# Sums of weight quarters made by accumulating transfers on POOL's queue instead of by VectorE

## The chip, the cores and the metric

The kernel runs on one core of one Trainium2 chip. The metric is the device time of one execution in microseconds; the number that counts is the median of several runs.

## The reference, cut to what matters

A block of a streaming encoder: 16 learned tokens are put ahead of 1024 frames of width 1024. A mixer (four mLSTM heads and four retention heads) is projected back by `w_out`; a gated MLP with a causal convolution over three tokens follows, whose last product is with `w_down`.

```python
mixed = jnp.concatenate([h_ml, h_rt], axis=-1)          # (L, 2048)
h = h + mixed @ w_out                                   # w_out (2048, 1024)
...
a = causal_dwconv(u @ w_up, ffn_conv_w)
h = h + (silu(a) * (u @ w_gate)) @ w_down               # w_down (2816, 1024)
```

All is float32. The change touches only how the two products with `w_out` and `w_down` get their weights.

## The kernel before, in words

**Stages.** The input is loaded and normed in four pieces of tokens (144, 256, 384, 256). Then the heads run one after the other in the order 4, 0, 1, 2, 3, 5, 6, 7: projections of values (`v_group`, L411), of queries and keys (`qk_group`, L447) and of the output gate (`o_group`), with the chunked scan of the head (`scan_a`, `scan_b`) merged in between. Up to about 700 us the trace shows this part, then the product with `w_out`, then the MLP from 840 us or so, and from about 1300 us the product with `w_down`. Each float32 operand is split into a high and a low half that TensorE takes as fp32r, so a product is three matmuls: high by high, high by low, low by high.

**Seven products for eight.** The products with `w_out` and `w_down` (class `Seven`, L630) are done by a Strassen scheme in Winograd's form: left and right factor are cut into quarters, and seven products of quarters, or of sums of quarters, take the place of eight. With w11, w21, w12, w22 the quarters of the weights, the scheme needs four sums of them: w21 + w22, w21 - w11, w21 + w22 - w11 and w12 - (w21 + w22 - w11). The activations need sums of their own (`tsum`, L681, and the step "65" in `prep`, L708 to L715). `give` (L746) and `last_quarter` (L752) add the products into the residual `resid`.

**Weight sums before.** They are made per row block of 128 (8 blocks for `w_out`, KD = 11 for `w_down`) and put into tensors in HBM, `sums[g, st, k]` (L183), two of them (`65` and `73`) of 128 x 1024 floats for each block. SP's queue brings the quarters into SBUF, VectorE makes the four sums, and SP's queue writes them to HBM. For `w_out` that is `wsum` (L185): two loads, four instructions on 128 x 512, four stores, tied by `after` behind the last instruction of a query or key group. For `w_down` it is done in halves, 22 units of two loads, four instructions on 128 x 256 and two stores (`dload`, `dsum`, `dnext`, `dstep`, L198 to L234), called from `seven` (L1335) in the MLP; their buffers are `Rb` and one tile `dsum`. `Seven.load` (L657) later reads the sums back as any weight, on SP's queue.

**Order of the work.** The program is recorded in the order of the Python code; a scheduling layer then orders each engine's instructions by the data they depend on and by its own estimate of the time, and sets the semaphores. `after` gives it an order that it must keep. `ahead` (L251 to L255) says behind which query or key group of which head a `wsum` or a `first_right` is called. POOL does almost nothing: memsets at the start (L383 to L401) and two multiplications at the end (L1576). SP issues nearly all transfers, in order; a load that waits holds up those behind it. At the start SP's queue holds, in this order: the first piece of the input (L106), the first head's value weights (L142), the second piece (L1004), constants, the third piece, the two rotary tables (L576, L577), the fourth piece, a mask, and the first query and key weights.

Of the kernel before, what the change touches and what calls it, by code (L numbers as in the profile page):

```python
# [10 lines left out]
F32 = mybir.dt.float32  # L11
F32R = mybir.dt.float32r
AF = mybir.ActivationFunctionType
ALU = mybir.AluOpType
# [3 lines left out]
P = 128  # L18
# [10 lines left out]
NPAIR = NFB // 2  # L29
# [35 lines left out]
def body(ctx, tc, h_in, vecs, cst, mask_in, rot, w_v0, w_v, w_fm, w_out, w_up, w_gate, w_down, out):  # L65
# [117 lines left out]
    sums = {(g, st, k): dram.tile([P, 2 * HB], F32, name=f"ws{g}{st}_{k}") for g, n in (("w", 8), ("d", KD)) for st in ("65", "73") for k in range(n)}  # L183

    def wsum(g, k):  # L185
        src, n = (w_out, 8) if g == "w" else (w_down, KD)
        a, b = (accp.tile([P, 2 * HB], F32, tag=f"rr{i}", name=f"ws{g}{k}_{i}") for i in range(2))
        nc.sync.dma_start(a, src[k])
        nc.sync.dma_start(b, src[k + n])
        w11, w21, w12, w22 = a[:, :HB], a[:, HB:], b[:, :HB], b[:, HB:]  # L190
        after(nc.vector.tensor_tensor(w22, w21, w22, ALU.add), last["qk"])
        nc.vector.tensor_tensor(w21, w21, w11, ALU.subtract)
        nc.vector.tensor_tensor(w11, w22, w11, ALU.subtract)
        nc.vector.tensor_tensor(w12, w12, w11, ALU.subtract)
        for st, i, x in (("65", 0, w11), ("65", 1, w22), ("73", 0, w12), ("73", 1, w21)):
            nc.sync.dma_start(sums[g, st, k][:, i * HB:(i + 1) * HB], x)

    def dload(k, q, x):  # L198

        n = HB // 2  # L200
        b = x.rearrange("p (a b j) -> p a b j", a=2, b=2)
        for i in range(2):
            nc.sync.dma_start(b[:, :, i], w_down[k + i * KD].rearrange("p (a j) -> p a j", a=2)[:, :, q * n:(q + 1) * n])

    def dsum(k, q, x, prev):

        n = HB // 2
        w11, w12, w21, w22 = (x[:, i * n:(i + 1) * n] for i in range(4))
        after(V.tensor_tensor(w22, w21, w22, ALU.add), prev)
        V.tensor_tensor(w21, w21, w11, ALU.subtract)  # L210
        V.tensor_tensor(w11, w22, w11, ALU.subtract)
        V.tensor_tensor(w12, w12, w11, ALU.subtract)
        for st, i, j in (("65", 0, 4), ("73", 1, 3)):
            nc.sync.dma_start(sums["d", st, k].rearrange("p (a j) -> p a j", a=2)[:, :, q * n:(q + 1) * n],
                              x.rearrange("p (i j) -> p i j", i=4)[:, i:j:3 if st == "65" else 1])

    dcount = [0, 0]
    dunits = [(k, q) for k in range(KD) for q in range(2)]
    dbufs = []

    def dnext():

        if len(dunits) > dcount[1]:
            x = dbufs[dcount[1] % 2] or fp4.tile([P, 2 * HB], F32, tag="dsum", name=f"dsum{dcount[1]}", bufs=1)
            dopen.append((*dunits[dcount[1]], x))
            dload(*dopen[-1])
            dcount[1] += 1

    dopen = []

    def dstep(x):
        if dopen:
            dsum(*dopen.pop(0), x)
            dnext()  # L234
# [6 lines left out]
    def first_right(k):  # L241
        a = accp.tile([P, 2 * HB], F32, tag="rr0", name=f"fr{k}")
        r = accp.tile([P, 2 * HB], F32R, tag="rr1", name=f"frs{k}")
        nc.sync.dma_start(a, mxd[k])
        nc.scalar.copy(r[:, :HB], a[:, :HB])
        after(nc.vector.tensor_tensor(r[:, HB:], a[:, :HB], r[:, :HB].bitcast(F32), ALU.subtract), last["qk"])
        nc.vector.tensor_tensor(a[:, HB:], a[:, HB:], a[:, :HB], ALU.subtract)
        nc.sync.dma_start(rone[k], r.bitcast(F32))
        nc.sync.dma_start(diff[k], a[:, HB:])

    ahead = {(g, "q", 0): [lambda k=k: wsum("w", k)] for k, g in enumerate((1, 2, 3, 5, 6, 7))}  # L251
    for k, g in ((6, 6), (7, 7)):
        ahead[g, "k", 1] = [lambda k=k: wsum("w", k)]
    for k in range(8):
        ahead[5 + k // 3, *(("q", 1), ("q", 2), ("k", 0))[k % 3]] = [lambda k=k: first_right(k)]  # L255

# [373 lines left out]
    class Seven:  # L630
# [48 lines left out]
                self.nload += 1  # L679

        def tsum(self, i, k):  # L681
            a, b, c = {1: ("A1", "B1", "A1"), 3: ("B1", "B1", "B2")}[i]
            return V.tensor_tensor(self.act[a, k], self.act[b, k], self.act[c, k], ALU.subtract)

        def prep(self, t):

            if t >= len(self.steps) or t in self.ops:
                return
            st, k = self.steps[t]
            nm = f"{self.nm}{st}_{k}"  # L690
            d = self.draws.get(t, {})
            act = self.act
            if st == "4" and self.order[-1] != "4":
                if t not in self.four:
                    self.pre4(t)
                r = rsplit(act["A1", k], self.rt(st, k, 0))
                self.ops[t] = [(self.four[t], r, "x")]
            elif st == self.order[-1]:
                if k % 2 == 0:
                    self.w = d.get("w")  # L700
                w = self.four.get(t) or wsplit(*self.wlast(k), [self.w[:, k % 2 * HB:(k % 2 + 1) * HB]])
                self.ops[t] = [(w, self.rhalf(k, 0), "xy"[st == "2"])]
            elif st in self.QUARTER:
                if k % 2 == 0:
                    self.w = fsplit(nm, [d["w"]])
                r = self.right.get((st, k)) or rsplit(act[{"1": "A1", "2": "A2", "4": "A1"}[st], k], self.rt(st, k, 0))
                self.ops[t] = [(half_of(self.w, k % 2), r, "xy"[st == "2"])]
            elif st == "65":  # L708
                a1, a2, b2 = (act[q, k] for q in ("A1", "A2", "B2"))
                r5 = rsplit(a1, self.rt(st, k, 1))  # L710
                V.tensor_tensor(a1, b2, a1, ALU.subtract)
                w = fsplit(nm, [d["l"]])
                r6 = rsplit(a1, self.rt(st, k, 0))
                V.tensor_tensor(a1, a2, a1, ALU.subtract)
                self.ops[t] = [(half_of(w, 0), r6, "x"), (half_of(w, 1), r5, "y")]  # L715
            else:
                w = fsplit(nm, [d["l"]])
                r7 = rsplit(act["B1", k], self.rt(st, k, 0))
                r3 = rsplit(act["B2", k], self.rt(st, k, 1))
                self.ops[t] = [(half_of(w, 1), r7, "x"), (half_of(w, 0), r3, "y")]  # L720
            self.read(t)
# [339 lines left out]
    for i, h in enumerate(HEADS):  # L1061
# [240 lines left out]
    def seven(kind, i, chunks, done):  # L1302
# [6 lines left out]
        for n, (bank, s, o, x) in enumerate(PROD):  # L1309
            hi, lo = need((kind, i, s), 2)  # L1310
            xs = xb(x)
            for ci, (j0, j1) in enumerate(chunks):
# [13 lines left out]
                if n in (0, 2, 3):  # L1326
                    if ci == 0:
                        S[n] = ftile(f"s{n}{kind}{i}")
                    nc.scalar.copy(S[n][:, w], pt)
                else:  # L1330
                    t = {1: 0, 4: 3, 5: 2}.get(n)
                    if t is not None:
                        x = nc.vector.tensor_tensor(S[t][:, w], pt, S[t][:, w], ALU.add)
                        if n != 4 and ci == len(chunks) - 1:
                            dstep(x)  # L1335
            if n == 1:
                done(0, 0, S[0])
            elif n == 4:
# [142 lines left out]
    for i in range(1, NPAIR):  # L1481
        u, g = up_part(i), gate_part(i)
        next(u)
        if i == 1:
            next(g)
        run(u)
        if i == NPAIR - 1:
            for t in range(4):
                down.load(t)
        run(g)  # L1490
        if 2 < i:
            kb = i - 3
            nc.sync.dma_start(resid[:, kb, META:], stream[:, kb])
        if i < 5:
            first_out((i - 1) % 2, (i - 1) // 2)
        if i == 4:
            fseg4.close()
            fp4 = fseg4.enter_context(tc.tile_pool(name="fp5", bufs=1, side="right"))
            dbufs += [Rb[:, :2 * HB], None]
            dnext()  # L1500
            dnext()

    for k in range(KD):
        aload("A1", k)
    down.prep(0)
    for k in range(KD - 1):
        aload("A2", k)
    assert not dopen
    fseg4.close()
    fseg2.close()  # L1510
    fseg.close()
# [172 lines left out]
```

## Time and profile before

| | |
|---|---|
| Median of 3 runs | 1537.58 us (1537.52 to 1537.78) |
| Span of the profiled execution | 1536.0 us |
| TensorE matmuls busy | 98% of the span |
| VectorE busy | 74% |
| ScalarE busy | 48% |
| POOL busy | 0%, 13 instructions |
| HBM read, written | 155.89 MB, 55.62 MB |
| Granted TensorE clock | 0.99 to 1.00 up to the last 16 us |

The span reaches from the first to the last instruction of the program in the profiled execution; what the runs have beyond it, 1.6 us, lies around it. A row of a group gives line, engine, operation, the tile written and the tiles read, the count, then busy time in us, the mean of one in ns, and the idle time of the engine ahead of it. A row of waits reads: who waited, for whom, us in total, times, the longest. In the rows of transfers stand the size of one in KB and the us from issue to landing.

### The profile page before, as it was taken

What the parts mean: (1) busy time and instruction counts of PE and PEld (TensorE: products, weight loads), DVE (VectorE), ACT (ScalarE), POOL (GpSimd) and SP (SyncE); (2) the same over time, 40 slices, a digit from 0 to 9 for tenths busy, and PEclk for the clock granted to TensorE, in tenths of its full rate; (3) what the DMA queues carried; (4) which work ended last, traced back from release to release, by engine and by line L of the source; (5) the groups of instructions that cost most, each with busy time, mean ns of one, the idle gap of its engine ahead of it and who ended that gap; (6) DMA issues with size and microseconds to landing.
All of it is one profiled execution on the core that took longest, in us unless ns stands there. A gap on an engine that the chain in (4) does not pass through costs nothing.

```text
span 1536.0 us, 25538 instructions
## 1 busy us (share of the span) xinstructions
PE 1512.7 (98%) x9753; PEld 1392.8 (91%) x9753; DVE 1131.5 (74%) x2443; ACT 743.2 (48%) x1491; POOL 2.5 (0%) x13
## 2 busy tenths in 40 slices
PE   7999999999999999999999999999999999999997
PEld 7989999999999999998788998999999999888887
DVE  8757767686867677687966788677777777778657
ACT  7374555555542534434454465444444444344443
POOL 0000000000000000000000000000000000000000
PEclk9999999999999999999999999999999999999999
DMA  6131231332425346278542245323465656933313
GB/s 216 42 98 63 70 122 65 109 112 80 141 67 184 126 131 209 91 249 305 184 146 97 83 129 181 102 93 101 155 193 167 198 186 230 366 109 104 96 42 111
DMA packets 111771, 213.18 MB, mean 139 GB/s; under 512 B 9944, under 2 KB 54688, under 8 KB 111648
## 3 DMA queue, kind: packets, MB, share of 16 engines
q1 hardware_dynamic: 111504, 211.48, 41.8%
q8 instruction: 76, 1.25, 0.3%
q14 instruction: 47, 0.39, 0.1%
q10 hardware_dynamic: 144, 0.07, 0.0%
HBM read 155.89 MB, written 55.62 MB: 138 GB/s over the span
## 4 chain that ended last, share of the span: by engine, by line
PE 95%; DMA 2%; DVE 2%; ACT 1%; issue 0%; DVEq 0%; ACTq 0%
PE pv L431 4%; PE pv L432 4%; PE pv L433 4%; PE po L442 4%; PE po L441 4%; PE po L443 4%; PE pdx L608 3%; PE pdx L610 3%; PE pdx L609 3%; PE pup_x L609 2%; PE pup_x L610 2%; PE pga_x L608 2%; PE pga_x L610 2%; PE pga_x L609 2%; PE pup_x L608 2%; PE pdy L608 2%
## 5 line engine op out<-in xcount | busy, mean ns | idle before, releaser
L431 PE MATMUL pv<-hi_v,uh 128*128 128x256 f32 (+1 forms) x512 | 147.2, 288 | 7.7 <-ACT hi_v L145 7.7
L432 PE MATMUL pv<-lo_v,uh 128*128 128x256 f32 (+1 forms) x512 | 145.9, 286 | 0.0
L433 PE MATMUL pv<-hi_v,ul 128*128 128x256 f32 (+1 forms) x512 | 145.6, 285 | 0.0
L441 PE MATMUL po<-uh,hi_o 128*128 128x386 f32 (+2 forms) x384 | 125.1, 326 | 0.0
L442 PE MATMUL po<-ul,hi_o 128*128 128x386 f32 (+2 forms) x384 | 122.8, 320 | 0.0
L443 PE MATMUL po<-uh,lo_o 128*128 128x386 f32 (+2 forms) x384 | 122.6, 319 | 0.0
L431 PEld LDWEIGHTS pv<-hi_v,uh 128*128 128x128 f32 x512 | 97.2, 190 | 10.5 <-ACT hi_v L145 7.7
L432 PEld LDWEIGHTS pv<-lo_v,uh 128*128 128x128 f32 x512 | 96.9, 190 | 0.9 <-DVE lo_v L146 0.8
L433 PEld LDWEIGHTS pv<-hi_v,ul 128*128 128x128 f32 x512 | 96.9, 190 | 0.1
L299 ACT CAST hi_up<-raw_up 128x512 fp32r<-128x512 f32 (+1 forms) x52 | 36.5, 719 | 105.7 <-PE pga_z L609 60.7
L441 PEld LDWEIGHTS po<-uh,hi_o 128*128 128x128 f32 x384 | 72.5, 189 | 0.1
L442 PEld LDWEIGHTS po<-ul,hi_o 128*128 128x128 f32 x384 | 72.4, 189 | 0.1
L443 PEld LDWEIGHTS po<-uh,lo_o 128*128 128x128 f32 x384 | 72.2, 188 | 0.1
L608 PE MATMUL pup_x<-uh_g,hi_up 128*128 128x256 f32 (+1 forms) x240 | 67.2, 282 | 0.4 <-ACT uh_g L1096 0.4
L609 PE MATMUL pup_x<-ul_g,hi_up 128*128 128x256 f32 (+1 forms) x240 | 67.4, 283 | 0.1
L610 PE MATMUL pup_x<-uh_g,lo_up 128*128 128x256 f32 (+1 forms) x240 | 66.3, 282 | 0.0
L300 DVE TENSOR_TENSOR lo_ga<-fraw_ga,hi_ga 128x512 fp32r<-128x512 f32 (+1 forms) x52 | 41.9, 808 | 32.2 <-ACT hi_ga L299 32.1
L300 DVE TENSOR_TENSOR lo_d<-rd,hi_d 128x1024 fp32r<-128x1024 f32 (+1 forms) x34 | 37.7, 1112 | 34.8 <-ACT hi_d L299 34.8
L441 PE MATMUL pq<-uh,hi_q 128*128 128x400 f32 (+2 forms) x192 | 62.1, 323 | 1.0 <-DVE qT L472 0.9
L442 PE MATMUL pk<-ul,hi_k 128*128 128x400 f32 (+2 forms) x192 | 62.1, 324 | 0.0
L441 PE MATMUL pk<-uh,hi_k 128*128 128x400 f32 (+2 forms) x192 | 62.0, 323 | 0.0
L443 PE MATMUL pq<-uh,lo_q 128*128 128x400 f32 (+2 forms) x192 | 62.0, 323 | 0.0
(757 smaller groups left out, 4978.7 us busy)
## 6 DMA issues: line engine op xcount, KB each, us to landing
raw_up<-w_up_d SPq DMA_DIRECT2D x22, 512.0 KB, 3.6
fraw_ga<-w_gate_d SPq DMA_DIRECT2D x22, 512.0 KB, 4.5
acts<-cv SPq DMA_DIRECT2D x44, 256.0 KB, 3.5
rd<-wsd SPq DMA_DIRECT2D x22, 512.0 KB, 3.5
raw_o<-w_fm_d SPq DMA_DIRECT2D x16, 512.0 KB, 3.5
wsw<-w_out_d SPq DMA_DIRECT2D x16, 512.0 KB, 3.8
wsw<-wsw SPq DMA_DIRECT2D x32, 256.0 KB, 2.1
raw_v<-w_v_d SPq DMA_DIRECT2D x14, 512.0 KB, 3.7
```

The lines of the kernel that those rows point to most:

```text
L299: nc.scalar.copy(hi[:, o:o + n], x)
L300: nc.vector.tensor_tensor(lo[:, o:o + n], x, hi[:, o:o + n].bitcast(F32), ALU.subtract)
L431: nc.tensor.matmul(pv[:L, :nv], a, hi[:, o:o + nv], start=kb == 0, stop=False)
L432: nc.tensor.matmul(pv[:L, :nv], a, lo[:, o:o + nv], start=False, stop=False)
L433: nc.tensor.matmul(pv[:L, :nv], b, hi[:, o:o + nv], start=False, stop=kb == KB - 1)
L441: nc.tensor.matmul(pt[:, :n], a, uh[kb][:, t0:t1], start=kb == 0, stop=False)
L442: nc.tensor.matmul(pt[:, :n], a, ul[kb][:, t0:t1], start=False, stop=False)
L443: nc.tensor.matmul(pt[:, :n], b, uh[kb][:, t0:t1], start=False, stop=kb == KB - 1)
L608: m.append(nc.tensor.matmul(pt, ah, xh_, start=first and k == 0, stop=False, skip_group_check=True))
L609: nc.tensor.matmul(pt, ah, xl_, start=False, stop=False, skip_group_check=True)
L610: m.append(nc.tensor.matmul(pt, al, xh_, start=False, stop=last and k == n - 1, skip_group_check=True))
```

## The change

One function `wsum(g, k)` makes the sums for both weights. It uses no SBUF and no VectorE: seven transfers on POOL's queue go from HBM to HBM, four of them accumulating (the target is read, the source added, the result written). Accumulation can only add here, so the sums are kept with plus signs only: the second half of `d65` becomes v21 + v22, where v are the quarters of the weights in the order of the listing, its first half v11 + v21 + v22, the second half of `d73` becomes v21 + v11, its first half v12 + v11 + v21 + v22. Where a sign has changed, the other factor is negated instead (`first_right`, `tsum`, step "65"), or the product is subtracted from the residual instead of added (`give`, `last_quarter`). What the mathematics needs of the original weights' signs comes out the same.

The first of the seven transfers waits for `last["pace"]`, an instruction of VectorE. `wsum("w", k)` is called at the same places as before; `wsum("d", k)` is called twice for each pair of the MLP, from pair 1, until the 11 blocks are used up. The transfers that follow the first are tied only by the data they read and write.

```diff
     def wsum(g, k):
+
         src, n = (w_out, 8) if g == "w" else (w_down, KD)
-        a, b = (accp.tile([P, 2 * HB], F32, tag=f"rr{i}", name=f"ws{g}{k}_{i}") for i in range(2))
-        nc.sync.dma_start(a, src[k])
-        nc.sync.dma_start(b, src[k + n])
-        w11, w21, w12, w22 = a[:, :HB], a[:, HB:], b[:, :HB], b[:, HB:]
-        after(nc.vector.tensor_tensor(w22, w21, w22, ALU.add), last["qk"])
-        nc.vector.tensor_tensor(w21, w21, w11, ALU.subtract)
-        nc.vector.tensor_tensor(w11, w22, w11, ALU.subtract)
-        nc.vector.tensor_tensor(w12, w12, w11, ALU.subtract)
-        for st, i, x in (("65", 0, w11), ("65", 1, w22), ("73", 0, w12), ("73", 1, w21)):
-            nc.sync.dma_start(sums[g, st, k][:, i * HB:(i + 1) * HB], x)
-
-    def dload(k, q, x):
...
+        d65, d73 = sums[g, "65", k], sums[g, "73", k]
+        v11, v21, v12, v22 = (src[k + i * n][:, o:o + HB] for i in range(2) for o in (0, HB))
+        dma = nc.gpsimd.dma_start
+        add = lambda x, y: dma(x, y, accum_op=ALU.add)
+        first = dma(d65, src[k])
+        tc.add_manual_dep(first.ins, last["pace"].ins.name, mybir.DependencyInfo(mybir.DependencyClass.Sync, mybir.DependencyReason.DATA), reason="pace")
+        dma(d73[:, HB:], v21)
+        dma(d73[:, :HB], v12)
+        add(d65[:, HB:], v22)
+        add(d73[:, HB:], v11)
+        add(d65[:, :HB], d65[:, HB:])
+        add(d73[:, :HB], d65[:, :HB])
...
-        nc.vector.tensor_tensor(a[:, HB:], a[:, HB:], a[:, :HB], ALU.subtract)
+        nc.vector.tensor_tensor(a[:, HB:], a[:, :HB], a[:, HB:], ALU.subtract)
...
-            a, b, c = {1: ("A1", "B1", "A1"), 3: ("B1", "B1", "B2")}[i]
+            a, b, c = {1: ("A1", "A1", "B1"), 3: ("B1", "B2", "B1")}[i]
...
-                V.tensor_tensor(a1, b2, a1, ALU.subtract)
+                V.scalar_tensor_tensor(a1, a1, -1.0, b2, ALU.mult, ALU.subtract)
...
-                V.tensor_tensor(a1, a2, a1, ALU.subtract)
+                V.scalar_tensor_tensor(a1, a1, -1.0, a2, ALU.mult, ALU.subtract)
...
-                    V.tensor_tensor(self.rs(j + j0, half), self.banks[b, j], self.rs(j + j0, half), ALU.add)
+                    x = self.rs(j + j0, half)
+                    V.tensor_tensor(x, x, self.banks[b, j], ALU.subtract if j0 else ALU.add)
...
-            V.tensor_tensor(x, pt, x, ALU.add)
+            V.tensor_tensor(x, x, pt, ALU.subtract if st == "4" else ALU.add)
...
                 qk_group(g, kind, p)
+                last["pace"] = last["qk"]
...
-                        x = nc.vector.tensor_tensor(S[t][:, w], pt, S[t][:, w], ALU.add)
-                        if n != 4 and ci == len(chunks) - 1:
-                            dstep(x)
+                        last["pace"] = nc.vector.tensor_tensor(S[t][:, w], pt, S[t][:, w], ALU.add)
...
         run(u)
+        if dsums and i < NPAIR - 1:
+            wsum("d", dsums.pop(0))
...
         run(g)
+        if dsums and i < NPAIR - 1:
+            wsum("d", dsums.pop(0))
```

The functions `dload`, `dsum`, `dnext` and `dstep` are gone, and with them the buffer `dsum` and the use of `Rb` for it.

More of the change, by code (lines that the diff above doesn't have):

```diff
@@ L194, in wsum @@
-        nc.vector.tensor_tensor(w12, w12, w11, ALU.subtract)
-        for st, i, x in (("65", 0, w11), ("65", 1, w22), ("73", 0, w12), ("73", 1, w21)):
-            nc.sync.dma_start(sums[g, st, k][:, i * HB:(i + 1) * HB], x)
-    def dload(k, q, x):
[L200 to L234, printed above, removed]
+        d65, d73 = sums[g, "65", k], sums[g, "73", k]
@@ L238, in body @@
+        add(d73[:, :HB], d65[:, :HB])
+    dcount = [0]
     rone = [dram.tile([P, 2 * HB], F32, name=f"rone{k}") for k in range(8)]
@@ L253, in body @@
         ahead[g, "k", 1] = [lambda k=k: wsum("w", k)]
+    dsums = list(range(KD))
     for k in range(8):
@@ L1498, in body @@
             fp4 = fseg4.enter_context(tc.tile_pool(name="fp5", bufs=1, side="right"))
-            dbufs += [Rb[:, :2 * HB], None]
-            dnext()
-            dnext()
     for k in range(KD):
@@ L1507, in body @@
         aload("A2", k)
-    assert not dopen
     fseg4.close()
```

## The prediction

> **What bounds the kernel now.** I read the page's first part, then TensorE's own waits, then busy time by stretches, and last the transfers of the start.
>
> ```profile
> span 1536.0 us, 25538 instructions
> PE 1512.7 (98%) x9753; PEld 1392.8 (91%) x9753; DVE 1131.5 (74%) x2443; ACT 743.2 (48%) x1491; POOL 2.5 (0%) x13
> ```
>
> ```profile
> PE pv L431 <- ACT hi_v L145: 7.7, 1, 7.7
> PE u L878 <- DVE C L916: 1.0, 1, 1.0
> PE pq L441 <- DVE qT L472: 0.9, 1, 0.9
> ```
>
> ```profile
> 0.00:5.00 5.00, 0.00 (x0) 0.00 (x0) 1.36 (x11) 2.52 (x7) 1.06 (x11) 1.00 0.65 183
> 5.00:10.00 5.00, 2.35 (x17) 0.89 (x17) 5.00 (x15) 4.20 (x12) 0.00 (x0) 1.00 1.03 361
> 10.00:15.00 5.00, 5.00 (x33) 4.91 (x30) 4.42 (x11) 4.08 (x11) 0.00 (x0) 1.00 1.07 397
> 15.00:20.00 5.00, 5.00 (x43) 5.00 (x43) 5.00 (x13) 4.50 (x11) 0.00 (x0) 1.00 1.06 388
> 20.00:25.00 5.00, 5.00 (x43) 4.84 (x42) 5.00 (x18) 4.85 (x13) 0.00 (x0) 1.00 0.59 223
> 25.00:30.00 5.00, 5.00 (x42) 4.83 (x41) 5.00 (x11) 5.00 (x12) 0.00 (x0) 1.00 0.00 0
> ...
> 150.00:900.00 750.00, 747.45 (x5078) 707.18 (x5077) 555.97 (x1337) 366.43 (x780) 0.00 (x0) 1.00 0.41 133
> 900.00:1500.00 600.00, 599.40 (x3463) 526.41 (x3462) 444.07 (x746) 275.32 (x487) 0.00 (x0) 1.00 0.48 155
> ```
>
> Columns of the last: length, then busy time and instructions of PE, PEld, DVE, ACT, POOL, then granted clock, DMA share and GB/s. TensorE is the bound: 1512.7 of 1536.0 us. It stands still 23.3 us: 7.7 before its first matmul, and between 150 and 1500 us 2.55 + 0.60 = 3.15. So whatever VectorE is relieved of, the middle can give back 3.15 us at most. The start is another matter. From 5 to 20 us the DMA engines are full (share 1.03 to 1.07, 361 to 397 GB/s), and TensorE, VectorE and ScalarE work right behind the data. Nowhere else in the quoted stretches is DMA the limit (shares 0.41 and 0.48).
>
> The sums below are made against the span of 1536.0 us; the median of the runs is 1537.58, so 1.6 us lie around the span, and I add them.
>
> **Removed: VectorE's additions.**
>
> ```profile
> L192 DVE TENSOR_TENSOR wsw<-wsw 128x512 f32<-128x512 f32 x8 | 5.5, 683 | 0.0
> L193 DVE TENSOR_TENSOR wsw<-wsw,wsw 128x512 f32<-128x512 f32 x8 | 5.4, 679 | 0.0
> L194 DVE TENSOR_TENSOR wsw<-wsw,wsw 128x512 f32<-128x512 f32 x8 | 5.4, 678 | 0.0
> L191 DVE TENSOR_TENSOR wsw<-wsw,wsw 128x512 f32<-128x512 f32 x8 | 5.4, 670 | 0.0
> L211 DVE TENSOR_TENSOR Rb<-Rb 128x256 f32<-128x256 f32 x11 | 4.6, 421 | 0.2
> ...
> L209 DVE TENSOR_TENSOR Rb<-Rb 128x256 f32<-128x256 f32 x11 | 4.6, 414 | 0.0
> ```
>
> For w_out 32 instructions, 21.7 us; for w_down eight such groups (four lines, two buffers) of 4.6, 36.8 us. VectorE loses 58.5 us, and SP's queue loses 136 transfers. What does TensorE gain? Only where it waits for a VectorE instruction that stands behind one of these. There is one clear place:
>
> ```profile
> 594.92 0.68 DVE L191 TENSOR_TENSOR wsw<-wsw,wsw 128x512 f32<-128x512 f32 x1
> 595.52 0.42 DVE L916 COPY C<-u 128x256 f32<-128x256 f32 x1
> ```
>
> The state copy L916, for which TensorE waits 1.0 us in the second view, stands behind L191. I book **-1.0 us**. From below the gain is 0, from above 3.15.
>
> **Signs.** tsum, give and last_quarter keep an instruction of the same kind. In step "65" a tensor_tensor becomes a scalar_tensor_tensor, 2 x (8 + 11) = 38 times.
>
> ```profile
> L711 DVE TENSOR_TENSOR wa<-wa,wa 128x512 f32<-128x512 f32 x8 | 5.5, 686 | 0.0
> ...
> L1352 DVE SCALAR_TENSOR_TENSOR cv<-c0b,vec,cv 128x512 f32<-128x512 f32 x8 | 5.9, 742 | 0.0
> ```
>
> 742 against 686 ns: 38 x 0.056 = 2.1 us of VectorE time, in stages where TensorE waits for nothing; **0**. Without that cover it would be 2.1.
>
> **Added: 133 transfers on POOL's queue**, seven for each of 19 units, all HBM to HBM: per unit a copy of 512 KB, two copies of 256 KB and four accumulating ones of 256 KB. Only the first of the seven (into d65) has the wait for "pace". The two copies into d73 and the accumulation of v11 onto the second depend on nothing that is computed. In the built program POOL's list therefore begins, behind eight memsets, with 57 = 3 x 19 of these transfers; the paced chains (copy, add, add, add, each waiting for the one before) come behind all of them. The first eight issue without a wait; from the ninth each waits for the transfer eight places before it. So up to eight 256 KB transfers, 2 MB, stand at the DMA engines from the first microseconds, and 57 x 256 KB = 14.9 MB are to be written before POOL turns to the chains.
>
> SP's queue at that time:
>
> ```profile
> resid<-h_in_d SPq DMA_DIRECT2D x2, 1024.0 KB, 7.5
> resid<-h_in_d SPq DMA_DIRECT2D x1, 1536.0 KB, 10.5
> raw_v<-w_v_d SPq DMA_DIRECT2D x4, 264.0 KB, 4.4
> A<-rot_d SPq DMA_DIRECT2D x2, 520.0 KB, 10.2
> ...
> resid<-h_in_d SPq DMA_DIRECT2D x2, 288.0 KB, 3.4
> ...
> cs<-cst_d SPq DMA_DIRECT2D x1, 134.0 KB, 7.2
> vec<-vecs_d ACTq DMA_DIRECT2D x1, 70.0 KB, 2.3
> ```
>
> Up to the last piece of the input that is 2x1024 + 1536 + 4x264 + 2x520 + 2x288 + 134 + 70 = 6460 KB = 6.61 MB. The stretches have moved 0.92 MB by 5 us, 2.72 by 10, 4.71 by 15, 6.65 by 20: the last input piece is there at 19.9 us. Now let POOL's transfers take half of the engines from 5 us on. SP gets half of 390, 195 GB/s, and the remaining 5.7 MB take 29.2 us: the last piece lands at 34.2 instead of 19.9.
>
> The Trainium skill, "DMA: Bandwidth & Descriptors", section "Issuing engines are not separate DMA queues", says that transfers of SP, ScalarE and GpSimd run on the same 16 engines and interleave. No run here shows both queues busy; if they were separate the start would cost nothing, which is the first rival. The same page, section "Queues, rings and completion order", says that an engine takes turns between the queues by packets; by that the half share would be the middle case, and rows shorter than POOL's 2 KB would push SP below it.
>
> What does TensorE make of it?
>
> ```profile
> L338 DVE SCALAR_TENSOR_TENSOR ul<-resid,vec,uh x32: 354/467/605, 4.9 to 27.5; 128x256 fp32r<-128x256 f32 x16, 128x144 fp32r<-128x144 f32 x8, 128x384 fp32r<-128x384 f32 x8
> ```
>
> ```profile
> L431 PE MATMUL pv<-hi_v,uh x64: 281/283/590, 7.7 to 36.1; 128*128 128x264 f32 x64
> ```
>
> The values' matmuls of all chunks now end at 36.4 us (last start 36.1 plus its two companions). A chunk has 24 of them, at 43 in 5 us (stretch 15 to 20) 2.8 us. The last two chunks need the last piece. From 34.2 its eight splits L338 take about 0.55 us each with the copies between, 4.4 us, during which the first chunk keeps pace; then its last matmuls and the second chunk follow: 34.2 + 0.9 + 4.4 + 2.8 = 42.3, and 0.5 for the norm's matmuls between. That is 42.8 against 36.4, **+6.4**. The norm of the last piece now comes right ahead of the projections that need it, where until now 7 us lay between; I add 0.6. **Start: +7.0.** The cover that hid TensorE from these loads was 10 us of data lying ahead; it is used up.
>
> Bounds by the share: with two thirds for SP (260 GB/s) the last piece lands at 5 + 21.9 = 26.9 and only the earlier pieces come 2 us late, about +2; with one third (130) at 48.8, so 57.4 for 42.8, +21. What a software-issued copy costs POOL is in no row. From below: slow issue leaves SP everything, 0; from above, the one third. I take half, with no row nearer to either end.
>
> **Later chains.** 19 chains of 512 + 3 x 256 KB in stretches at DMA shares of 0.41 and 0.48 while some 40 MB of SP's old transfers are gone (19 units, 1 MB read and 1 MB written for each). POOL itself owes the others only the memset of vh's ones column, which stands behind 17 of the transfers and is first read by the second head's scan, and at the end two multiplications. SP reads the sums, in order, so that a late sum would hold all loads behind it:
>
> ```profile
> 658.61 0.56 DVE L472 TENSOR_TENSOR kT<-pk,A 128x384 f32<-128x384 f32 x1
> ```
>
> ```profile
> L657 SPq DMA_DIRECT2D rd<-wsd x22: 319/320/339, 1343.1 to 1455.2; - x22
> L657 SPq DMA_DIRECT2D wdh<-wsw x6: 319/320/423, 732.3 to 771.8; - x6
> ...
> L657 SPq DMA_DIRECT2D raw_w<-wsw x4: 319/348/842, 703.3 to 715.9; - x4
> ```
>
> The last w_out chain is released at 658.6. At the longest landing of the start's rows, 10.5 us, four transfers take 42 us and end near 701; the sums of that unit are read after 732. Cost **0**.
>
> **Sum:** 1536.0 - 1.0 + 0 + 7.0 + 0 = 1542.0, with 1.6 around it **1543.6 us**.
>
> **Rivals.**
> First, the burst is hidden: POOL issues so slowly, or the engines serve SP so much, that SP keeps two thirds or more. For it: POOL has done nothing but memsets so far, and its rate is unknown. Against: eight transfers may stand at once, and the DMA share is over 1. Time: 0 to +2 less 1.0, 1537.6 to 1538.6, say 1538.2.
> Second, POOL takes two thirds, since its rows are 2 KB and an accumulation must also read its target: +21 - 1, 1557.6. Against: the copies must go through HBM both ways, which may slow them.
> Third, faster: VectorE's relief is worth more, at one place, the middle: all 3.15 us of TensorE's idle time between 150 and 1500 us hang on VectorE's queue and go, while the first POOL copy reaches the engines only after 20 us: 1537.6 - 3.2 = 1534.4. It decides once SP's last input piece lands no later than 20 us. Against: of the waits listed there few end at VectorE, and POOL is free from 1.5 us on.
> Fourth, the pacing does harm: accumulations are so slow that SP stands at the sums. It needs a chain of over 73 us (658.6 to 732), 18 us for each of four; each further microsecond adds one; a chain of 85 us gives 1537.6 + 12, 1549.6.
>
> **How the numbers follow.** Forecast 0.50, hidden 0.23, two thirds 0.15, faster 0.08, pacing 0.04. A measurement of this kernel tells 0.2%, 3.1 us, from no change: under 1534.5 faster, up to 1540.7 the same. Faster 0.08, same 0.23, slower 0.50 + 0.15 + 0.04 = 0.69. The forecast's own range, shares of 0.4 to 0.6 for SP, is 1539 to 1551. The range leaves out the faster case and the lower end of the hidden one (0.10 together), and the upper part of the two thirds (0.08): 1536.6 to 1556.5.
>
> **What would show it.** Right: in the first 60 us the POOL queue moves some MB; SP's input pieces land after 25 us, not 20; TensorE's idle time before 45 us grows by 5 to 9 us, and from 150 us on the time from stage to stage is that of before within 2 us; VectorE loses some 56 us of busy time. The wait of 1.0 us for C is gone. Wrong: the DMA share between 5 and 20 us is made by SP alone (hidden), the last input piece lands after 45 us (two thirds), or SP waits at L623 for POOL (pacing). If the start is unchanged and the time still differs, my reading of the middle as saturated is what failed.

## The result and the profile after

The changed kernel takes 1572.0 us (median of 3 runs, 1569.48 to 1577.59) against 1537.58: ratio 1.0235, 95% interval 1.0205 to 1.0264. It is 34.4 us slower. The forecast was 1543.6 us with a range up to 1556.5; the direction and the first of two places were right; the size was not, and some 7 to 10 us were lost at a place for which the forecast had nothing.

The profiled execution of the changed kernel took 1577.59 us, the longest of the three; its span is 1575.8 us. First part of its page:

```profile
span 1575.8 us, 25378 instructions
PE 1526.8 (97%) x9753; PEld 1400.9 (89%) x9753; DVE 1088.6 (69%) x2323; ACT 746.7 (47%) x1495; POOL 94.8 (6%) x146
HBM read 175.82 MB, written 75.54 MB: 160 GB/s over the span
```

VectorE lost 42.9 us of busy time and the kernel gained nothing from it. TensorE's waits show a new kind at the top, the splits of the input (`uh`, the lines that read `resid`), 15.2 us in three waits:

```profile
PE pv L397 <- DVE uh L301: 8.4, 2, 6.6
PE pv L397 <- ACT hi_v L145: 8.1, 1, 8.1
PE pv L397 <- ACT uh L303: 6.8, 1, 6.8
```

Where the time is lost, by stretches (columns as in the prediction):

```profile
5.00:10.00 5.00, 1.89 (x9) 0.67 (x9) 3.94 (x12) 3.29 (x10) 1.56 (x5) 1.00 1.02 375
10.00:15.00 5.00, 3.32 (x16) 2.34 (x15) 1.82 (x3) 1.26 (x2) 2.39 (x5) 1.00 1.08 399
15.00:20.00 5.00, 3.92 (x19) 2.63 (x18) 0.43 (x1) 0.37 (x1) 2.53 (x6) 1.00 0.98 292
20.00:25.00 5.00, 0.00 (x0) 0.00 (x0) 0.00 (x0) 0.00 (x0) 2.64 (x5) 0.63 1.05 359
25.00:30.00 5.00, 4.27 (x19) 4.28 (x20) 4.23 (x11) 3.92 (x10) 1.05 (x2) 0.50 0.95 221
...
45.00:50.00 5.00, 1.53 (x11) 1.29 (x10) 0.00 (x0) 0.00 (x0) 1.23 (x3) 0.86 1.03 353
50.00:55.00 5.00, 1.61 (x6) 1.34 (x7) 2.35 (x8) 2.35 (x6) 2.19 (x4) 0.50 1.00 259
55.00:60.00 5.00, 5.00 (x29) 5.00 (x29) 4.99 (x11) 4.71 (x13) 2.31 (x4) 0.61 0.71 151
...
150.00:900.00 750.00, 742.28 (x5000) 701.08 (x4999) 535.04 (x1297) 368.47 (x771) 23.67 (x32) 1.00 0.41 126
900.00:1500.00 600.00, 596.83 (x3518) 527.68 (x3518) 417.41 (x675) 271.78 (x488) 32.59 (x44) 1.00 0.49 141
```

From 20 to 25 us TensorE, VectorE and ScalarE do nothing (POOL's 2.64 us are its issues of transfers) while the DMA engines are full (share 1.05): 1.17 of the 1.80 MB that they move are POOL's. And the middle, where TensorE stood still for 3.15 us before, now loses 7.7 + 3.2 = 10.9 us.

A ruler for the rest: the first start of the queries' matmul, which TensorE does behind the values of the whole input. Before, then after:

```profile
L441 PE MATMUL pq<-uh,hi_q x192: 276/337/445, 38.2 to 648.3; 128*128 128x400 f32 x64, 128*128 128x384 f32 x64, 128*128 128x256 f32 x64
```

```profile
L407 PE MATMUL pq<-uh,hi_q x192: 276/338/450, 63.8 to 684.1; 128*128 128x400 f32 x64, 128*128 128x384 f32 x64, 128*128 128x256 f32 x64
```

38.2 became 63.8: 25.6 us are lost before the first query. The last start is late by 35.8, so the next 10 us go between the first head and the last.

**The start, on SP's queue.** SP's issues at the start, before (start, duration, line, what):

```profile
5.75 3.32 SPq L576 DMA_DIRECT2D A<-rot_d  x1
9.11 0.44 SPq L577 DMA_DIRECT2D A<-rot_d  x1
9.59 0.55 SPq L1004 DMA_DIRECT2D resid<-h_in_d  x1
```

The same three in the chain of work that ended last, after, where the landing follows:

```profile
9.05 13.20 SPq L542
...
22.77 29.86 DMA resid<-h_in_d
```

Two delays are read here. SP's issue of the first rotary table takes 13.2 us instead of 3.3. It looks as if SP's queue took no more until older transfers had moved; the trace names no reason. So the last piece of the input is issued at 22.8 instead of 9.6 us. And from there it takes 29.9 us to land, at 52.6.

**The second place, at `first_right`.** VectorE in the changed kernel, 264 to 273 us:

```profile
264.04 0.62 DVE L433 SCALAR_TENSOR_TENSOR cvk<-rk,vec,cvk 128x400 f32<-128x400 f32 x1
272.31 0.69 DVE L212 TENSOR_TENSOR fr<-fr 128x512 f32<-128x512 f32 x1 [7.64 <-DMA fr<-mxd]
272.92 0.16 DVE L944 COPY mm<-mx 128x2 f32<-128x2 f32 x1
```

VectorE stands 7.64 us in front of a load that SP issued at 265.7, and what TensorE needs stands behind it in VectorE's queue. The groups of that line, before and after:

```profile
L247 DVE TENSOR_TENSOR fr<-fr 128x512 f32<-128x512 f32 x8 | 5.5, 688 | 4.4 <-DMA fr<-mxd 4.4
```

```profile
L212 DVE TENSOR_TENSOR fr<-fr 128x512 f32<-128x512 f32 x8 | 5.5, 689 | 18.3 <-DMA fr<-mxd 18.1
```

VectorE's wait grew from 4.4 to 18.1 us, ScalarE's for the same loads from 27.4 to 51.0. The loads themselves, before and after (KB, median us from issue to landing):

```profile
fr<-mxd SPq DMA_DIRECT2D x8, 512.0 KB, 3.7
```

```profile
fr<-mxd SPq DMA_DIRECT2D x8, 512.0 KB, 6.5
```

### The profile page after: what moved, and what is told of

It reads as the page before. It is cut to its first block, busy times and chain, and to the rows that moved or that the text cites. A ratio compares the mean times of both kernels' runs of the same rounds, so it can differ in the third digit from the quotient of the medians.

```text
span 1575.8 us, 25378 instructions
## 1 busy us (share of the span) xinstructions
PE 1526.8 (97%) x9753; PEld 1400.9 (89%) x9753; DVE 1088.6 (69%) x2323; ACT 746.7 (47%) x1495; POOL 94.8 (6%) x146
## 4 chain that ended last, share of the span: by engine, by line
PE 86%; DMA 6%; DVE 3%; ACT 2%; SPq 1%; issue 1%; DVEq 0%; ACTq 0%
PE pv L397 3%; PE pv L398 3%; PE pv L399 3%; PE po L407 3%; PE po L408 3%; PE po L409 3%; PE pdx L574 3%; PE pdx L576 3%; PE pdx L575 3%; PE pup_x L575 2%; DMA fr<-mxd 2%; PE pup_x L576 2%; PE pga_x L574 2%; PE pga_x L576 2%; PE pga_x L575 2%; PE pup_x L574 2%
## 5 line engine op out<-in xcount | busy, mean ns | idle before, releaser
L398 PE MATMUL pv<-lo_v,uh 128*128 128x256 f32 (+1 forms) x512 | 149.1, 292 | 0.0
L265 ACT CAST hi_up<-raw_up 128x512 fp32r<-128x512 f32 (+1 forms) x52 | 36.4, 719 | 108.1 <-PE pga_z L575 61.1
L266 DVE TENSOR_TENSOR lo_up<-raw_up,hi_up 128x512 fp32r<-128x512 f32 (+1 forms) x52 | 41.2, 808 | 35.2 <-ACT hi_up L265 34.4
```

Source lines behind the costliest of these rows:

```text
L265: nc.scalar.copy(hi[:, o:o + n], x)
L266: nc.vector.tensor_tensor(lo[:, o:o + n], x, hi[:, o:o + n].bitcast(F32), ALU.subtract)
L398: nc.tensor.matmul(pv[:L, :nv], a, lo[:, o:o + nv], start=False, stop=False)
```

## The experiments

Theory: the 57 untied transfers, three of each unit, start in the first microseconds and take the DMA engines from SP's input (some 25 us); a second, smaller part comes later, at `first_right`. Rivals: the burst's later effects cost as well; the paced chains cost by bandwidth wherever they run; the negated factors or the order of instructions cost. Each kernel is compared with the kernel before, run beside it on the same chip (its median there: 1536.5 to 1537.7). "First query" is the start of the first queries' matmul, 38.2 us before.

| | us, median (range) | ratio, 95% interval | first query |
|---|---|---|---|
| 1 all root transfers tied | 1544.47 (1541.42 to 1546.94) | 1.0049 (1.0035 to 1.0063) | 38.7 |
| 2 burst alone, memsets behind it | 1575.8 (1573.68 to 1576.58) | 1.0249 (1.0235 to 1.0263) | 73.0 |
| 3 same, rows of 1 KB | 1623.33 (1618.59 to 1624.15) | 1.055 (1.0532 to 1.0568) | 117.7 |
| 4 as 1, first_right's load tied | 1546.91 (1544.4 to 1548.98) | 1.0065 (1.0052 to 1.0077) | 39.1 |
| 5 burst alone, behind the memsets | 1559.51 (1556.32 to 1562.37) | 1.0145 (1.0124 to 1.0166) | 62.1 |
| 6 as 5, rows of 1 KB | 1545.59 (1543.99 to 1549.29) | 1.0057 (1.004 to 1.0075) | 42.4 |
| 7 as 1, first_right in two halves | 1551.81 (1548.0 to 1554.66) | 1.0093 (1.0071 to 1.0115) | 37.9 |
| 8 as 1, no sums for w_out | 1534.5 (1533.86 to 1538.38) | 0.9984 (0.9975 to 0.9994) | 38.9 |
| 9 as 4, chains for w_out early | 1537.35 (1535.03 to 1538.96) | 1.0 (0.9991 to 1.0009) | 38.6 |
| 10 as 1, rows of 1 KB | 1544.04 (1540.52 to 1546.13) | 1.0041 (1.0026 to 1.0056) | 39.1 |
| 11 burst alone, from 45 us on | 1547.89 (1545.92 to 1549.82) | 1.0074 (1.0057 to 1.009) | 37.8 |
| 12 as after, chains for w_out early | 1560.86 (1559.33 to 1562.04) | 1.0159 (1.0144 to 1.0174) | 60.3 |
| 13 as 5, at most three open | 1548.95 (1546.9 to 1550.72) | 1.0071 (1.0055 to 1.0087) | 41.3 |
| 14 as 5, at most one open | 1542.55 (1541.13 to 1545.23) | 1.0034 (1.0024 to 1.0044) | 37.3 |

**1. The burst taken away.** From the changed kernel:

```diff
-        first = dma(d65, src[k])
-        tc.add_manual_dep(first.ins, last["pace"].ins.name, ...)
-        dma(d73[:, HB:], v21)
-        dma(d73[:, :HB], v12)
+        for first in (dma(d65, src[k]), dma(d73[:, HB:], v21), dma(d73[:, :HB], v12)):
+            tc.add_manual_dep(first.ins, last["pace"].ins.name, ...)
```

> Burst theory: the 57 transfers that wait for nothing cost the start 28 us of the 34; with all three root transfers of each unit tied to the pace, the last input piece lands near 20 us again, not at 52.6, the first query projection starts near 38 us, not at 63.8, and the time is 1572 - 28 = 1544 (1540 to 1548); what is left over 1537.6 is the moved order of first_right and the chains. Rival (the accumulating transfers as such, or the order of the work, make it slow): the time stays above 1560.

1544.47: of 34.4 us some 27 go, and the first query is back at 38.7. VectorE and the sign changes are those of the changed kernel, so they are not the cause of these. 7.7 us stay, all of them between 240 and 700 us; in the MLP and the product with `w_down`, where 11 chains run, this kernel keeps a constant distance of 9.2 us (profiled execution) to the kernel before. The chains for `w_down` cost nothing there.

**2 and 3. The burst alone, into spare tensors, from the kernel before.** In the second the rows are 1 KB.

```diff
+    for g, src, n in (("w", w_out, 8), ("d", w_down, KD)):
+        for k in range(n):
+            t = dram.tile([P, 2 * HB], F32, name=f"spare{g}{k}")
+            nc.gpsimd.dma_start(t[:, HB:], src[k][:, HB:])
+            nc.gpsimd.dma_start(t[:, :HB], src[k + n][:, :HB])
+            nc.gpsimd.dma_start(t[:, HB:], src[k][:, :HB], accum_op=ALU.add)
```

> The kernel before with nothing but 57 untied transfers of 256 KB of the same forms added, into spare tensors that nobody reads; the sums are still made by VectorE. Burst theory: the start loses what it loses in the changed kernel, first query projection near 64 us, time 1537.6 + 26 to 29 = 1563.6 to 1566.6. Rival (the start alone is not enough, later chains and order cost as much): under 1555.

> As the burst alone, but every transfer is cut into rows of 1 KB instead of 2 KB, same bytes in all. If the engines take turns by rows or packets, so that the row length sets the share, POOL's share falls: last input piece at 36 to 42 us instead of 52, time 1546 to 1553. If the share does not follow the row length (turns by bytes or by the time an engine needs), the time is that of the burst with 2 KB rows within 3 us, or longer.

Neither is the test it was meant to be. Standing ahead of POOL's memsets, the burst held up the memset of `Rc`, to 63.7 us in the second and to 105.3 in the third, and TensorE stood behind it. TensorE's waits in the second:

```profile
PE pra L370 <- DVE Rc L365: 9.4, 1, 9.4
```

In the third that wait is 71.5 us. What they do show: a transfer that POOL can't issue keeps a memset of a tenth of a microsecond waiting for tens of them.

**4. `first_right`'s load held back,** as in the first, with

```diff
-        nc.sync.dma_start(a, mxd[k])
+        x = nc.sync.dma_start(a, mxd[k])
+        tc.add_manual_dep(x.ins, last["qk"].ins.name, ...)
```

> As the one with all transfers tied, and the loads of first_right tied to the query or key group behind which they are called. Theory of the order: the 7 us lost near 265 us came from VectorE standing 7.6 us at a first_right load that had moved forward since its buffer is free now; with it tied the time is 1537 to 1540, VectorE's relief worth at most 1 us. Rival (the paced chains take bandwidth from SP's loads): no better than all tied alone, 1543 or more.

1546.91, no better. The loss at 250 to 300 us is gone (the queries that start at 298.4 us before are 1.2 us late instead of 3.3), but 7 us are lost from 552 to 644 us instead. To hold back a load so that nobody stands at it early doesn't help when it then lands late.

**5 and 6. The burst behind the memsets,** with rows of 2 KB and of 1 KB (the same loop, each transfer ordered behind POOL's last memset; in the sixth each moves 256 rows of 1 KB).

> The kernel before, and the burst of transfers alone: 57 untied transfers of 256 KB with rows of 2 KB on the POOL queue, 19 of them accumulating, into spare tensors that nothing reads, tied to POOL's last memset so that every memset stands ahead of them (in the earlier run with the burst alone, memsets stood behind it and TensorE waited some 9 us for Rc on top). The weight sums stay on VectorE as before. Theory A (the burst delays SP's input pieces and costs the start, nothing else): the first query-key matmul 25 to 28 us later than before, last input piece near 52 us, time 1562 to 1566. Theory B (the burst of the changed kernel costs all of its 34 us, by what it leaves behind as well): 1569 to 1573. If SP's share is half, as the prediction had it: 1544 to 1546.

> As the run before it, but each of the 57 transfers goes in 256 rows of 1 KB in place of 128 of 2 KB; bytes and transfers are the same, and the memsets stand ahead of it. Theory A (the queues take turns by row, so that the share goes by row length): POOL's and SP's shares near half each, SP's last input piece lands at 26 to 35 us, the first query-key matmul 3 to 10 us later than before, time 1540 to 1548. Theory B (the share goes by queue or by transfers in flight, whatever the row): as with rows of 2 KB, 1562 to 1566. The burst itself should last longer than with 2 KB rows, and nothing reads it.

The fifth gives 1559.5, 22 us; the first query is 23.9 us late and from 129 us on no more is lost. That is theory A, a little under its range. The sixth gave what theory A expected of it (first query 4.2 us late, 1545.6). But its trace spoils the reading: with 1 KB rows POOL issued three transfers and stopped for 4.4 us, with 2 KB seven. Row length and number of open transfers had changed together, so two more runs were made. The packets in the two traces say more: the plain copies went in packets of 4 KB in both, and only the accumulating transfers changed, from 2 to 1 KB. So for two thirds of POOL's bytes the cut into rows of 1 KB changed no packet.

**13 and 14. Rows of 2 KB, three or one open.** From the fifth, in the same loop, with n = 3 or 1:

```diff
+                if len(spare) >= n:
+                    tc.add_manual_dep(x.ins, spare[-n].ins.name, ...)
```

> The kernel before and the 57 transfers with rows of 2 KB into spare tensors, behind the memsets as in the fifth experiment, but each issued only when the transfer three places before it has landed, so that at most three stand at the DMA engines where there were seven (with rows of 1 KB there were three as well). Theory A (POOL's share goes by row length): as the fifth experiment, the first query-key matmul 20 us or more late, 1556 to 1562. Theory B (it goes by how many transfers stand open): as with rows of 1 KB, the first query-key matmul 3 to 8 us late, 1541 to 1548.

> The same with each transfer issued only when the one before it has landed, so that one stands open. Theory A: SP's last input piece still lands over 45 us while the burst lasts, 1550 to 1560. Theory B: the first query-key matmul 0 to 3 us late, 1537 to 1543.

Theory A (row length) falls as the cause. With rows of 2 KB and three open the first query is 3.1 us late, less than with 1 KB rows; with one open it isn't late. (The time of 13 lies 1 us above theory B's range.) The queues between 5 and 40 us (transfers' packets, MB, share of 16 engines; q0 is POOL's, q1 SP's), for the fifth, the thirteenth and the fourteenth:

```profile
q0 software_dynamic: 2427, 7.55, 62.0%
q1 hardware_dynamic: 3203, 4.97, 40.8%
```

```profile
q1 hardware_dynamic: 4666, 7.50, 58.8%
q0 software_dynamic: 1329, 3.49, 35.3%
```

```profile
q1 hardware_dynamic: 4679, 7.54, 59.2%
q0 software_dynamic: 639, 1.64, 19.0%
```

What POOL gets falls with the number of transfers that it has open: 62, 35, 19%. With seven open SP moves 4.97 MB in these 35 us, with three or one 7.5, which is nearly all that it had to move. From 5 to 25 us, while SP had work in all of them, POOL had 63, 32 and 12% of the engines and SP moved 2.65, 5.34 and 6.76 MB. The sixth, with three open and rows of 1 KB, has 32% and 5.33 MB there: the same as the thirteenth. A slower burst lasts longer: the last of the 57 is issued at 83.5 us in the fifth, 130.2 in the thirteenth, 152.0 in the sixth, 261.0 in the fourteenth. So the rest of what 6, 13 and 14 cost (8.2, 11.3 and 4.9 us in all) comes after the first query, most of it while the burst still runs beside later loads; in 13 some 3 us more come in the MLP, which no theory here explains.

**11. The burst from 45 us on,** tied to the first query group.

> The kernel before and the same burst of 57 transfers with rows of 2 KB into spare tensors as in the fifth experiment, but tied to the last VectorE step of the first query group, so that it starts near 45 us, after the input pieces have landed, and lasts to some 110 us. Theory A (the burst costs what it takes from loads that TensorE waits for, above all the input pieces): the first query-key matmul as before, later loads of the second head and of the first VectorE sums late by some us, time 1537 to 1547. Theory B (16 MB on the POOL queue cost their time wherever they lie): 1556 to 1562, as the fifth experiment.

1547.9, 11.4 us: half of what the burst costs at the start, and just above theory A's range. The first query is on time (37.8), but 10.7 us are lost by 139 us. The queues from 40 to 120 us, and a piece of its chain:

```profile
q0 software_dynamic: 5068, 13.66, 70.1%
q1 hardware_dynamic: 3432, 5.16, 20.9%
```

```profile
88.51 12.11 DMA A<-scr
```

One of two loads of 512 KB for the scan (`A` from `scr`) takes 12.1 us to land.

**7. `first_right` cut in two.** As the first; the load of piece k at one query or key group, its copy, subtractions and stores at the next.

```diff
+        if k:
+            a = frb[k - 1]
...
+            after(nc.vector.tensor_tensor(r[:, HB:], a[:, :HB], r[:, :HB].bitcast(F32), ALU.subtract), last["qk"])
+            after(nc.vector.tensor_tensor(a[:, HB:], a[:, :HB], a[:, HB:], ALU.subtract), last["qk"])
...
+        if k < 8:
+            frb[k] = accp.tile([P, 2 * HB], F32, tag="rr0", name=f"fr{k}")
+            x = nc.sync.dma_start(frb[k], mxd[k])
```

> The kernel with all three root transfers of each unit tied (1544.5, first experiment), and first_right cut in two: the load of piece k is tied to one query-key group, its ACT copy, both VectorE subtractions and stores to the next one. Theory A (the rest of the loss, some 7 us, is ACT and VectorE standing in order at loads that were only just issued, with PE behind them): the waits of VectorE and ACT on fr fall from 17 and 49 us to under 3 and 10, and the time to 1536 to 1539. Theory B (the loss is bandwidth that the chains of POOL take from SP's loads): 1542 to 1546, waits on fr small but PE late on other loads.

A miss, 1551.8. ScalarE still stands 61.0 us at these loads and VectorE 13.6. A head's three query groups take some 13 us (from the queries' to the keys' first matmul), so one group is 4 to 5 us; the loads land in 3.0 to 8.0 us. One group of lead isn't enough, and ScalarE's copy, which no order ties, is moved up to the load:

```profile
680.38 0.62 ACT L210 CAST frs<-fr 128x512 fp32r<-128x512 f32 x1 [11.11 <-DMA fr<-mxd]
```

This run doesn't tell the two theories apart.

**8. No sums for `w_out`.**

```diff
+        if g == "w":
+            return
...
-                nc.sync.dma_start(x[:, :2 * HB], sums[self.nm, st, k])
+                nc.sync.dma_start(x[:, :2 * HB], self.wd[k] if self.nm == "w" else sums[self.nm, st, k])
```

> The same kernel with all root transfers tied, but the sums of the w_out quarters are left out altogether: 56 transfers on the POOL queue fewer, and the output projection reads the plain quarters of w_out where it read the sums; first_right is as in the first experiment. Theory A (ACT and VectorE stand in order at first_right's loads, whatever POOL moves): the loss between 298 and 690 us stays, 1543 to 1546. Theory B (bandwidth taken by the chains for w_out): the loss goes, 1535 to 1538, and first_right's loads land in 3.7 us as before the change and not in 6.6.

1534.5: the loss is gone without a change at `first_right`. VectorE's wait there is 7.5 us instead of 17.3. So the chains for `w_out` are needed for it; an order at `first_right` alone is not the cause. This kernel does less work, so that 0.16% below the kernel before is no gain.

**9. The chains moved away from `first_right`.** As the fourth, and

```diff
-    ahead = {(g, "q", 0): [lambda k=k: wsum("w", k)] for k, g in enumerate((1, 2, 3, 5, 6, 7))}
-    for k, g in ((6, 6), (7, 7)):
-        ahead[g, "k", 1] = [lambda k=k: wsum("w", k)]
+    ahead = {(k // 2, *(("q", 0), ("k", 1))[k % 2]): [lambda k=k: wsum("w", k)] for k in range(8)}
```

> All root transfers tied and first_right's load tied, as in the fourth experiment, and the eight chains for w_out moved from the head groups 1, 2, 3, 5, 6, 7 to the groups 0, 1, 2, 3 (two in each), so that none runs beside first_right's loads of groups 5 to 7. Theory A (the 7 to 10 us left are the chains beside first_right's loads, where ACT and VectorE stand in order): fr's loads land in 2 to 4.4 us, ACT's waits on fr fall from 50 to 30 us, no loss between 550 and 700 us, time 1534 to 1538. Theory B (a chain costs wherever it lies beside SP's loads): the loss moves to the groups before 410 us, time 1541 to 1547.

1537.35, ratio 1.0 (0.9991 to 1.0009): the whole rest is gone, with the same chains at another place. VectorE's wait at `first_right`, this kernel:

```profile
L211 DVE TENSOR_TENSOR fr<-fr 128x512 f32<-128x512 f32 x8 | 5.5, 686 | 0.4 <-DMA fr<-mxd 0.4
```

The loads land in 3.5 us at the median. Theory B, that a chain costs wherever it lies, falls.

**12. The burst kept, only the chains moved.** The ninth with the first transfer alone tied, as in the changed kernel.

> The changed kernel with its burst kept (only the first root transfer of each unit is tied), and only the second part undone: the chains for w_out moved to the groups 0 to 3, and first_right's load tied. If the two parts of the loss stand side by side, 34 less 7 to 10: 1561 to 1565, the start 24 to 28 us late and nothing lost from 200 us on. If they overlap: 1567 or more.

1560.86: 24.4 us. In its profiled execution the distance to the kernel before stays between 21 and 24 us from 130 us to 700, where the changed kernel's grows from 27 to 37. The two parts stand side by side: 24.4 (burst, chains moved) and 7.7 (no burst, chains in place), 32.1 together, against 34.4 (31.5 to 40.6 by the ratio's interval).

**10. All paced, rows of 1 KB.** As the first, each transfer cut into column halves.

> All root transfers tied as in the first experiment, first_right and the places as there, but every transfer of the sums is cut into column halves, so that its rows are 1 KB and not 2 or 4 KB (twice the transfers, the same bytes). Theory A (the share of the DMA engines goes by row length, at the chains as at the start): first_right's loads land in 3.5 to 5 us and not 6.6, most of the 7 us go, time 1536 to 1540. Theory B (the chains cost by transfers or bytes, not by rows): 1543 to 1548.

By the median 1544.04, theory B; the load's landing fell only from 6.6 to 5.9 us. Its runs spread over 5.6 us, so that a gain of one or two can't be excluded. By the trace three quarters of the chains' bytes went in shorter packets than in the first (1 KB for 2 in the accumulating transfers, 4 KB for 32 in the copy of 512 KB), so their length isn't what decides at the chains.

## Why the prediction was wrong, point by point

**What bounds the kernel: right.** TensorE is the bound, VectorE's relief can give little back, and the start is the place where transfers count. Number nine has the whole change with both losses mended: VectorE works 1089.7 us instead of 1131.5 and the time is that of before.

**VectorE's additions, -1.0: not found.** The wait for C is gone from the list, but in nine the interval of the ratio leaves room for 1.4 us either way. The gain is between nothing and that. VectorE's busy time fell by 42.9 us, not by some 56. The durations of the rows add up to more than the busy time since instructions overlap: L191 at 594.92 with 0.68 ends after L916 starts at 595.52. If each of the 120 removed instructions overlapped by these 0.08 us, an estimate from this one pair, that is 9.6 of the 13 us; the rest is not traced.

**Signs, 0: right.** The new instruction in step "65" takes what the old one took, and not 742 ns (changed kernel; 686 and 683 for the lines of before):

```profile
L680 DVE SCALAR_TENSOR_TENSOR wa<-wa,wa 128x512 f32<-128x512 f32 x8 | 5.4, 680 | 0.0
L677 DVE SCALAR_TENSOR_TENSOR wa<-wa,wa 128x512 f32<-128x512 f32 x8 | 5.4, 678 | 0.0
```

**The start, +7.0: the step that failed.** "SP gets half of 390, 195 GB/s, and the remaining 5.7 MB take 29.2 us: the last piece lands at 34.2". It landed at 52.6. The queues between 5 and 53 us, changed kernel:

```profile
q0 software_dynamic: 3162, 9.61, 59.0%
q1 hardware_dynamic: 4530, 6.98, 43.7%
```

SP moved 6.98 MB in 48 us, 145 GB/s. So SP's rate was 145 for 195 (1.34 times as long): it got 42% of the bytes, and both together moved 346 GB/s, not 390. And the last piece was not alone: 6.98 MB went by for 5.7 (1.22 times), since the first weights for queries and keys, 1 MB, were issued at 36.7 and 38.3 us and moved beside it. 29.2 x 1.34 x 1.22 = 47.7, and 5 + 47.7 = 52.7. (The rest of the extra bytes are the mask, and 0.2 MB that SP had moved less by 5 us.) The share by itself was not the largest of these: 42% for a half makes 1.19, 346 for 390 GB/s makes 1.13, the bytes 1.22; the share alone would have put the landing near 40 us. What followed the landing was reckoned well: the prediction's end of the values, 8.6 us behind the last piece, gives 61.2 for 36.4, +24.8; the last of these matmuls starts at 62.1 for 36.1, and the first query was 25.6 late. The bound "one third" (landing at 48.8, +21) was the nearest case. The prediction had seen in the built program that eight transfers could stand open (seven did) and then took turns by queue, though the share goes with the number of open transfers: runs 5, 13 and 14.

The Trainium skill, "DMA: Bandwidth & Descriptors", section "Queues, rings and completion order", has an engine take turns between the queues by packets. The prediction drew from it that SP's shorter rows would push its share below half. SP's share is below half here, 42%, as that rule has it, though POOL's plain copies went in packets of 4 KB and not of 2; but run 13, with the same packets, gives SP the greater part. Whether POOL's queue ran empty at some engines between its issues there, so that the rule still holds, no run shows.

**Later chains, 0: the second step that failed, by 7.7 to 10 us.** It asked when SP would stand at the sums, and found rightly that it doesn't. It did not ask which engines stand in order at other loads of SP while a chain runs. Taking `wsum` off the buffer that `first_right` uses let the first of these loads be issued near 240 us (265.7 in the changed kernel) for 480.2 before, with VectorE's second subtraction, which nothing ties, behind it. And each chain ran beside the rest of them. Runs 8 and 9 show that the chains' place decides it.

**Rivals.** Of the named ones, "POOL takes two thirds" (1557.6, chance 0.15) comes nearest at the start, by the time of the landing (its sign, later than 45 us, came true) and not by its reason: SP's 42% of the bytes lie within the forecast's own 0.4 to 0.6. With the landing as measured the sum would have been 1536.0 - 1 + 25.6 + 1.6 = 1562, and run 12 has 1560.9. The second loss was in no rival. The fourth rival, SP at the sums, didn't occur.

**Open.** How much of the loss is the clock. In the changed kernel's trace TensorE's granted clock fell to 0.50 at 21.3 and at 48.6 us, for 10.2 us each time. Between 25 and 60 us its busy time times the missing part of the clock is 5.8 us, an estimate of the most that it cost, part of it beside waits for data. Reckoned the same way up to 1500 us it is 10.0 us, for 1.7 in the kernel before; in the first experiment it is 4.6, since the clock is halved for 6.8 us behind a standstill of 3.5 us at 598. So up to 8 of the 40 us that the changed kernel's profiled execution loses, and up to 3 of the 9 us that the first experiment's loses, may be matmuls done at half clock. No run takes the clock's part by itself.

Also open is a loss at the start of the MLP, ahead of the first paced chain for `w_down` (976.5 us in the changed kernel). Where the kernel before is between 870 and 935 us, the changed kernel's profiled execution loses 4.6 us; runs 12 and 13 lose 2 to 3 there, run 1 nothing. No run shows the cause.

## What to carry to other kernels

A transfer that depends on nothing starts when its queue reaches it, and a queue that did nothing reaches it in the first microseconds (1.4 us here): in a chain of transfers every root needs the pacing, not only the first in the code. What the background transfers took here from the loads that matter went with how many of them stood open at once, so limit these, or keep them away from stretches in which an engine stands in order at a load. Before counting what an engine is relieved of, look whether the bound waits for it: 42 us off VectorE were worth nothing here.

## What the runs showed of the hardware beyond that

- SP's own issue stalled while the DMA engines were full: 13.2 us in one instruction (3.3 before), so that loads far down its queue were late twice, at the issue and at the landing.
- POOL issued seven transfers of 256 KB with 128 rows of 2 KB at once, but only three of 256 rows of 1 KB, and then stopped; the record of a plain issue is mostly 0.5 to 0.6 us long, that of an accumulating one some 0.8.

```profile
L191 POOL DMA_DIRECT2D wsw<-w_out_d x16: 802/826/895, 14.6 to 703.4; - x16
L191 POOL DMA_DIRECT2D wsw<-wsw x16: 802/812/836, 258.3 to 713.3; - x16
```

- TensorE's granted clock went to half 2.4 and 2.1 us into two standstills of 6.8 and 6.6 us (changed kernel, 18.9 and 46.5 us). It was also halved for 3.4 us at 822 us in the kernel before, where the trace shows no pause between matmuls. The Trainium skill, "TensorE: Matmul & The Clock Gate", section "Part 1: The HAM clock gate (the "warmup" mystery)", says that the clock is halved after an idle window of some 3.4 us. The two long standstills agree in the main, though the clock fell after less than that; the drop at 822 us does not.
